# Four narrow merge-gate blocks as a twelfth block of the seven-product stage, with two more mLSTM heads' q and k in front of it

## The chip, the cores and the metric

The program runs on one core of a Trainium2 chip, in one launch. A core has engines that run side by side, each through its own list of instructions in order: TensorE (PE, matrix products into PSUM), VectorE (DVE), ScalarE (ACT), GpSimd (POOL) and SyncE (SP, which here only issues DMAs; ACT and POOL issue some too). They wait for each other through semaphores. The metric is the device time of one execution, in microseconds (us), lower is better.

## The reference, cut to what matters

A decoder layer with two token mixers side by side: 512 tokens, width 2048, all in float32. One projection of the normalised input `u` is cut into the inputs of both mixers and of the two merge gates:

```
u = _rmsnorm(h, norm_w)
proj = jnp.matmul(u, w_in)
(ml_q, ml_k, ml_v, ml_o, ml_z, ml_i, ml_f,
 dn_qkv, dn_z, dn_b, dn_a, gate_a, gate_b) = jnp.split(proj, idx, axis=-1)
h_a = _mlstm_chunkwise(q, k, v, i_pre, logf)         # 8 heads, q and k 128 wide, v 256 wide
h_a = _rmsnorm(h_a) * ml_norm_w * sigmoid(ml_o) * silu(ml_z)
h_b = _gated_delta_chunkwise(dq, dk, dv, beta, g)    # 16 heads of 128, after a causal conv and silu
h_b = _rmsnorm(h_b, dn_norm_w) * silu(dn_z)
y_a = jnp.matmul(h_a, w_out[:ML_WIDTH]); y_b = jnp.matmul(h_b, w_out[ML_WIDTH:])
return sigmoid(gate_a) * y_a + sigmoid(gate_b) * y_b  # added to h, then a last RMSNorm
```

`gate_a` and `gate_b` are 4096 columns of the projection; `ml_q` and `ml_k` are 1024 each.

## The kernel before, in words

Every large product is made of three: weights and `u` are split into a high part (rounded, `wh`, `uh`) and a rest (`wl`, `ul`), and high x high, high x rest and rest x high are added in PSUM. The split of a weight tile is one copy on ACT (`split_hi`, L136) and one subtraction on DVE (`split_lo`, L139). Weight tiles of 256 KB come in through the tag `wr` (four buffers, loads four tiles ahead, splits three ahead) in the order of the list `plan`.

There are three ways to project columns. `proj_cm` gives 256 columns as channels x tokens: 8 weight tiles, 96 matmuls that stream 512 columns each (L258 to L260). `proj_tm` gives 256 columns as tokens x channels: 8 weight tiles, 192 matmuls that stream 256 columns each (L273 to L276). `seven_stage` gives 1024 columns as tokens x channels with seven products of half-size blocks in place of eight: 336 matmuls that stream 512 columns each (L610 to L612), and on DVE and ACT the sums of weight blocks and of results that this needs. Its helper `sink_flat` puts the gates through tanh and stores them in `tg_d`.

The program's stages, in order on PE:

1. The front: `u` is made; mLSTM's q, then k, of heads 0 and 1 by `proj_cm` (stored in `qk_d` by `spill`); then the first two narrow merge-gate blocks (`narrow_gates`, `proj_tm`, 256 columns each). Beside them run `gates` (the small per-head gates), `u_sums` (sums of blocks of `u` for the seven products) and `lead` (the first weights of the next stage).
2. The seven-product stage: 11 blocks, listed in `SEVEN`: four `z`, two `s`, two `v`, three `g` (gates from column 1024 on).
3. The mixers: eight units (`dn_unit`), each two DeltaNet heads. A unit projects k, v and q of its heads (three `proj_cm` blocks); units 1 to 6 have one more `proj_cm` block behind k, which projects q and k of one mLSTM head (2 to 7) and starts `ml_head`. Heads 0 and 1 are started by `ml_first`, which loads q and k from `qk_d`.
4. The other two narrow merge-gate blocks, by `proj_tm`.
5. The output projection of `h_a`: four narrow `proj_tm` blocks (`n`), two wide blocks (`o`), and the seven-product stage again for `h_b` (two blocks).

PE's order is the order of the program. What runs beside the projections is written as generators: each calls for a pause of some steps, and a step passes with every 6 matmuls of `proj_cm` and every 12 of `proj_tm`, so that a block has 16 steps. `start(gen, wait)` sets the first step. The order on DVE, ACT, POOL and SP comes from a scheduler that takes priorities (`urgent`, `behind`) into account. Buffers limit it: an mLSTM head has one buffer each for q and k (`mkq`), for v and for its weights, and shares with the DeltaNet heads two buffers `g` for the gate.

What the change and the prediction touch, step by step:

- PSUM tag `pj` has three buffers and each `proj_cm` block takes two, so the second half of a block's first step needs the block before it copied out. For k, v and q of a unit that copy is `yp<-pj` on ACT (L831).
- `travel` (L867) stores transposed tiles by four DMAs of 64 KB; an mLSTM head stores its result `hm_d` by eight of them, a unit its `h_d` by eight per pair of heads, all on ACT's queue, in order with ACT's other work.
- `dn_front_k` inverts, on DVE, by 31 pairs of small operations (`tmp`, L942, and `xi`, L944); then the result goes through DRAM (`xd`, `tt`) and is transposed (`tn`, L960). 25 steps behind the end of the q block (9 where the unit has an mLSTM block) `dn_back` uses `tn` on PE (L998).
- `load_h` reads `hm_d` back in 16 tiles (`hr`, in the buffers of `wr`) and puts their high parts and rests into `uh` and `ul` (ACT L1238, DVE L1239), over those of `u`, for the output projection.
- `close` opens the buffers for the last stage when no generator is left; it is asked behind each `n` block.

## Time and profile before

| what | value |
|---|---|
| median of 3 runs | 2251.95 us (2249.82 to 2252.3) |
| the profiled execution's own time, as its span | 2252.6 us |
| DVE busy | 1658.0 us (74%) |
| ACT busy | 944.6 us (42%) |
| POOL busy | 294.0 us (13%) |
| front, to the first seven-product matmul | 0 to 126.7 us |
| seven-product stage, 11 blocks | 126.7 to 986.5 us |
| mixers, eight units | 986.5 to 1808.6 us |
| two narrow merge-gate blocks | 1808.6 to about 1864 us |

An execution of this program was taken with the hardware profiler; its span, from the first to the last instruction, is the time that the profile accounts for. Busy shares are per engine. A matmul's own duration in the profile overlaps the next one's, so PE's time per matmul is read from the distance of starts. "Idle before" is time in which an engine waited, with what ended the wait. The limits of the stages are starts of matmuls of the lines named above.

### The profile page before, as it was taken

The page shows a single profiled execution, that of the slowest core. Times are in us where ns is not written, and L with a number is a line of the kernel's source. Part 1 is how long each engine was busy: PE and PEld are TensorE (multiplying, and loading weights), DVE is VectorE, ACT ScalarE, POOL GpSimd, SP SyncE. Part 2 cuts the span into 40 slices and gives each one's busy share as a digit, 9 for nine tenths or more (in the row PEclk, how much of TensorE's full clock was granted, in tenths as well). Part 3 has the DMA queues.
Part 4 walks back from the last instruction along what each step waited for, and adds up shares of the span by engine and source line. Part 5 has one row for each costly group of instructions (what it writes and reads, how often), then busy time and mean ns, then how long its engine had stood idle before and what let it go on. Part 6 is the DMA issues. An engine that isn't in the chain of part 4 may idle for free. (4 is left out here: it accounts for less than half of the span.)

```text
span 2252.6 us, 33199 instructions
## 1 busy us (share of the span) xinstructions
PE 2183.0 (97%) x11408; PEld 1822.1 (81%) x11408; DVE 1658.0 (74%) x2911; ACT 944.6 (42%) x1824; POOL 294.0 (13%) x362
## 2 busy tenths in 40 slices
PE   7999999999999999998999999999999999999986
PEld 5987888788778778887888888888888899987765
DVE  5787888778877777857786777777767765747777
ACT  4444444445444444433434434343443443323334
POOL 0420000000000000012322131221222110000124
PEclk9999999999999999999999999999999999999988
DMA  5456666567667776767666665757666565958686
GB/s 159 129 166 198 212 202 209 191 194 239 201 202 225 229 222 189 247 195 181 154 162 152 145 167 131 176 136 172 138 167 147 134 172 171 284 155 258 206 238 243
DMA packets 541131, 422.27 MB, mean 187 GB/s; under 512 B 241441, under 2 KB 417794, under 8 KB 540962
## 3 DMA queue, kind: packets, MB, share of 16 engines
q1 hardware_dynamic: 443426, 358.20, 56.7%
q10 hardware_dynamic: 95744, 57.76, 8.4%
q0 software_dynamic: 1792, 4.20, 0.8%
q8 instruction: 89, 1.46, 0.3%
q14 instruction: 80, 0.66, 0.1%
HBM read 335.03 MB, written 85.00 MB: 186 GB/s over the span
## 5 line engine op out<-in xcount | busy, mean ns | idle before, releaser
L136 ACT CAST wh<-wr 128x512 fp32r<-128x512 f32 (+1 forms) x576 | 396.2, 690 | 554.1 <-PE pj L259 275.3
L139 DVE TENSOR_TENSOR wl<-wr,wh 128x512 fp32r<-128x512 f32 (+1 forms) x576 | 479.9, 836 | 178.7 <-ACT wh L136 168.6
L258 PE MATMUL pj<-uh,wh 128*128 128x512 f32 x1024 | 429.9, 420 | 5.5 <-ACT yp L831 5.5
L260 PE MATMUL pj<-uh,wl 128*128 128x512 f32 x1024 | 401.5, 392 | 0.0
L259 PE MATMUL pj<-ul,wh 128*128 128x512 f32 x1024 | 400.5, 391 | 0.0
L611 PE MATMUL ps<-wl,uh 128*128 128x512 f32 x592 | 234.0, 395 | 6.5 <-DVE wl L139 6.4
L610 PE MATMUL ps<-wh,uh 128*128 128x512 f32 x592 | 232.8, 393 | 6.0 <-DVE X L670 5.6
L612 PE MATMUL ps<-wh,ul 128*128 128x512 f32 x592 | 231.1, 390 | 0.0
L260 PEld LDWEIGHTS pj<-uh,wl 128*128 128x128 f32 x1024 | 192.8, 188 | 43.2
L258 PEld LDWEIGHTS pj<-uh,wh 128*128 128x128 f32 x1024 | 193.8, 189 | 40.5 <-ACT yp L831 5.9
L259 PEld LDWEIGHTS pj<-ul,wh 128*128 128x128 f32 x1024 | 194.0, 189 | 33.1
L136 ACT CAST wh<-ts 128x512 fp32r<-128x512 f32 x200 | 123.4, 617 | 222.1 <-DVE ts L568 180.5
L136 ACT CAST wh<-t 128x1024 fp32r<-128x1024 f32 x104 | 109.5, 1053 | 245.1 <-PE ps L612 115.0
L611 PE MATMUL ps<-wl,suh 128*128 128x512 f32 x528 | 205.7, 390 | 0.5 <-DVE wl L139 0.5
L610 PE MATMUL ps<-wh,suh 128*128 128x512 f32 x528 | 205.9, 390 | 0.0
L612 PE MATMUL ps<-wh,sul 128*128 128x512 f32 x528 | 205.5, 389 | 0.0
L139 DVE TENSOR_TENSOR wl<-t,wh 128x1024 fp32r<-128x1024 f32 x104 | 132.0, 1269 | 42.7 <-ACT wh L136 42.0
L139 DVE TENSOR_TENSOR wl<-ts,wh 128x512 fp32r<-128x512 f32 x200 | 139.1, 699 | 31.3 <-ACT wh L136 31.3
L273 PE MATMUL pjt<-wh,uh 128*128 128x256 f32 x512 | 147.6, 288 | 0.8 <-ACT tgs L787 0.7
L275 PE MATMUL pjt<-wl,uh 128*128 128x256 f32 x512 | 144.8, 283 | 0.0
L276 PE MATMUL pjt<-wh,ul 128*128 128x256 f32 x512 | 144.8, 283 | 0.0
L611 PEld LDWEIGHTS ps<-wl,uh 128*128 128x128 f32 x592 | 111.4, 188 | 38.7 <-DVE wl L139 17.0
(321 smaller groups left out, 3845.1 us busy)
## 6 DMA issues: line engine op xcount, KB each, us to landing
wr<-in_w_in_dram SPq DMA_DIRECT2D x680, 256.0 KB, 3.7
wr<-in_w_out_dram SPq DMA_DIRECT2D x144, 256.0 KB, 4.3
t_d<-ts ACTq DMA_DIRECT2D x88, 256.0 KB, 4.3
wr<-t_d SPq DMA_DIRECT2D x88, 256.0 KB, 4.0
wr<-in_w_in_dram SPq DMA_DIRECT2D x96, 128.0 KB, 3.1
xt<-in_x_dram SPq DMA_DIRECT2D x8, 512.0 KB, 8.1
v<-v_d SPq DMA_DIRECT2D x8, 512.0 KB, 6.2
gb<-rows_d SPq DMA_DIRECT2D x16, 256.0 KB, 4.7
```

The lines of the kernel that those rows point to most:

```text
L136: newest["A"] = A.copy(hi, src).ins
L139: newest["V"] = V.tensor_tensor(out=lo, in0=src, in1=hi.bitcast(F32), op=ALU.subtract).ins
L258: T.matmul(ps[j], hi[:, k, wsl], uh[:, kt, :], start=(kt == 0), stop=False)
L259: T.matmul(ps[j], hi[:, k, wsl], ul[:, kt, :], start=False, stop=False)
L260: T.matmul(ps[j], lo[:, k, wsl], uh[:, kt, :], start=False, stop=(kt == KT - 1))
L273: T.matmul(o, uh[:, kt, tsl], hi[:, k, :], start=(kt == 0 and c % 2 == 0), stop=False, skip_group_check=True)
L275: T.matmul(o, uh[:, kt, tsl], lo[:, k, :], start=False, stop=False, skip_group_check=True)
L276: T.matmul(o, ul[:, kt, tsl], hi[:, k, :], start=False, stop=(kt == KT - 1), skip_group_check=True)
L610: T.matmul(ps[t], ah, hi, start=(g == "A" and i == 0), stop=False, skip_group_check=True)
L611: T.matmul(ps[t], ah, lo, start=False, stop=False, skip_group_check=True)
L612: T.matmul(ps[t], al, hi, start=False, stop=(i == KH - 1), skip_group_check=True)
```

## The change

The four narrow merge-gate blocks (gate columns 0 to 1023) are gone; `SEVEN` has a fourth `g` block, so that the seven-product stage has 12 blocks. In the front, where two of the narrow blocks stood, q and k of mLSTM heads 2 and 3 are projected by `proj_cm` and stored in `qk_d`. Units 1 and 2 have no mLSTM block any more; heads 2 and 3 are started by `ml_first` too, and the four heads of `ml_first` start at steps 1, 41, 81 and 121 of the mixers (before: two, at 1 and 45). The longer pause of head 2 (`late`) is gone. Behind the mixers PE goes straight to the `n` blocks, and `load_h` starts in front of the last unit's q block (before: in front of the last narrow gate block, two blocks later).

```diff
--- before.py
+++ after.py
@@ -24,8 +24,7 @@
 NRAW, NSPL = 4, 4
 RAHEAD, SAHEAD = 4, 3
 PRIO = 1500
-GFIRST = 2
-GNARROW = 4
+QKFIRST = 2
 YNARROW = 4
 GLAG = 8
 HP = S // 2
@@ -45,12 +44,12 @@
 NSYS = 32
 
 
-UNITS = [(p, p + 1 if 0 < p < 7 else None) for p in range(8)]
+UNITS = [(p, p + 1 if 2 * QKFIRST - 2 < p < 7 else None) for p in range(8)]
 
 SEVEN = ([("z", ML_Z + c, ML_O + c) for c in range(0, D, NO)]
          + [("s", DN_Z + c, DN_Z + c + NO) for c in range(0, D, 2 * NO)]
          + [("v", ML_V + c, ML_V + c + NO) for c in range(0, D, 2 * NO)]
-         + [("g", GATE + c, GATE + c + NO) for c in range(GNARROW * NB, 2 * D, 2 * NO)])
+         + [("g", GATE + c, GATE + c + NO) for c in range(0, 2 * D, 2 * NO)])
 
 
 @with_exitstack
@@ -86,7 +85,7 @@
     v_d = dr.tile([NC, P, D], F32, tag="vd", name="v_d")
     g_d = dr.tile([NC, P, D], F32, tag="gd", name="g_d")
     gz_d = dr.tile([NC, P, D], F32, tag="gzd", name="gz_d")
-    qk_d = dr.tile([4, P, S], F32, tag="qkd", name="qk_d")
+    qk_d = dr.tile([4 * QKFIRST, P, S], F32, tag="qkd", name="qk_d")
 
     ident = cp.tile([P, P], F32, tag="ident", name="ident")
     make_identity(nc, ident)
@@ -143,18 +142,13 @@
         return tc.issue_after(newest[eng])
 
 
-    def add_gates(blocks):
-        for b in blocks:
-            plan.extend(("i", GATE + b * NB, k) for k in range(0, KT, KP))
-
-    plan = [("i", c, k) for c in (ML_Q, ML_K) for k in range(0, KT, KP)]
-    add_gates(range(GFIRST))
+    QK = [(a, b) for b in range(QKFIRST) for a in range(2)]
+    plan = [("i", (ML_Q, ML_K)[a] + b * NB, k) for a, b in QK for k in range(0, KT, KP)]
     nfront = len(plan)
     for p, h in UNITS:
         for kind, c in (("i", DN_K + p * NB), ("m", h), ("i", DN_V + p * NB), ("i", DN_Q + p * NB)):
             if c is not None:
                 plan += [(kind, c, k) for k in range(0, KT, KP)]
-    add_gates(range(GFIRST, GNARROW))
     plan += [("n", b * NB, k) for b in range(YNARROW) for k in range(0, KT, KP)]
     plan += [("o", nb * NO, k) for nb in range(YNARROW * NB // NO, D // NO) for k in range(KT)]
     raws, parts = [], []
@@ -779,20 +773,11 @@
     lead, seven = seven_stage(sbp, (suh, sul), (s4h, s4l), X, t2_d, w_in, 0, SEVEN, SINK, begin_mixers)
 
 
-    def narrow_gates(b):
-        ps = proj_tm(GATE + b * NB)
-        for i in range(2):
-            tg = wp.tile([P, 2, NB], F32, tag="tg", name="tgs", bufs=3)
-            with urgent():
-                A.activation(tg, ps[i], AF.Tanh, scale=0.5)
-            nc.sync.dma_start(tg_d[2 * i:2 * i + 2, :, b * NB:(b + 1) * NB].rearrange("c p n -> p c n"), tg)
-
     start(gates())
     start(u_sums(), 11)
     start(lead(), 38)
-    spill(proj_cm(ML_K), 2, 1.0)
-    for b in range(GFIRST):
-        narrow_gates(b)
+    for a, b in QK[1:]:
+        spill(proj_cm((ML_Q, ML_K)[a] + b * NB), 2 * QKFIRST * a + 2 * b, 1.0 if a else float(P) ** -0.5)
     for b, blk in enumerate(SEVEN):
         seven(2 * KH * b, *blk)
     while active:
@@ -1112,13 +1097,15 @@
                 A.mul(mkq[:, 1, :], ps[0], float(P) ** -0.5)
             with urgent():
                 A.copy(mkq[:, 0, :], ps[1])
-            start(ml_head(mh, mkq, 16 if p == 1 else 0), 1)
+            start(ml_head(mh, mkq), 1)
         ps = proj_cm(DN_V + dcol)
         for j in range(2):
             vt = wk.tile([P, NC, P], F32, tag="vn", name="vt", bufs=4)
             u["vs"].append(vt)
             conv_silu(ps[j], 32 + hs[j], vt.rearrange("p c t -> p (c t)"))
             start(silu_end(vt.rearrange("p c t -> p (c t)"), (vt, vt)), 4 + 3 * j)
+        if p == UNITS[-1][0]:
+            start(load_h(hm_d, lambda k: 16 + k, 1, False), 4)
         ps = proj_cm(DN_Q + dcol)
         u["qn"] = []
         for j in range(2):
@@ -1129,7 +1116,7 @@
         start(dn_front_q(hs, kq, u), QWAIT)
         start(dn_back(hs, kq, u), 25 if mh is None else 9)
 
-    def ml_head(h, kq, late):
+    def ml_head(h, kq):
         kT, qT = kq[:, 0, :], kq[:, 1, :]
         kw = wk.tile([P, NC, P], F32, tag="mkw", name="kw", bufs=1)
         with behind("V"):
@@ -1162,7 +1149,7 @@
         v1 = wk.tile([P, NC, NB + 1], F32, tag="mv1", name="v1", bufs=1)
         G.memset(v1[:, :, NB:NB + 1], 1.0)
         nc.sync.dma_start(v1[:, :, 0:NB], v_d[:, :, h * NB:(h + 1) * NB].rearrange("c p n -> p c n"))
-        yield 6 + late
+        yield 6
         with behind("V"):
             V.tensor_tensor(out=kw, in0=kw, in1=bc(we, P), op=ALU.mult)
         yield 2
@@ -1217,18 +1204,10 @@
 
         kq = wk.tile([P, 2, S], F32, tag="mkq", name="mkq", bufs=1)
         for i in range(2):
-            nc.sync.dma_start(kq[:, 1 - i, :], qk_d[2 * i + h])
+            nc.sync.dma_start(kq[:, 1 - i, :], qk_d[2 * QKFIRST * i + h])
         yield 4
-        yield from ml_head(h, kq, 0)
-
-    start(ml_first(0), 1)
-    start(ml_first(1), 45)
-    for unit in UNITS:
-        dn_unit(*unit)
-
-
-
-    hh, hl = {0: uh}, {0: ul}
+        yield from ml_head(h, kq)
+
     y_d = dr.tile([NC, P, D], F32, tag="yd", name="y_d")
 
     def load_tile(dst, src):
@@ -1247,10 +1226,10 @@
             split_scaled(uh[:, k, 0:n], ul[:, k, 0:n], raw[:, 0:n], normc[:, norm(k):norm(k) + 1])
             yield step
 
-    for b in range(GFIRST, GNARROW):
-        if b == GNARROW - 1:
-            start(load_h(hm_d, lambda k: 16 + k, 1, False), 4)
-        narrow_gates(b)
+    for h in range(2 * QKFIRST):
+        start(ml_first(h), 1 + 40 * h)
+    for unit in UNITS:
+        dn_unit(*unit)
 
     h1s, h2s = ctx.enter_context(ExitStack()), ctx.enter_context(ExitStack())
     late = {}
```

ACT at the third mLSTM head's store. Before, this is head 2 (the one of unit 1), while unit 2 runs; the `w` are copies of the DeltaNet chain, `mkq` takes q and k of the next head out of PSUM:

```order
L867 DMA hm_d<-to 32x16x32
L1062 COPY w<-pw 128x128
L867 DMA hm_d<-to 32x16x32 x2
L1062 COPY w<-pw 128x128
L867 DMA hm_d<-to 32x16x32
L136 CAST wh<-wr 128x512
L867 DMA hm_d<-to 32x16x32 x4
L136 CAST wh<-wr 128x512 x2
L1062 COPY w<-pw 128x128
L1112 ACTIVATE mkq<-pj 128x512
L1062 COPY w<-pw 128x128
```

Now it is head 2 again, now in unit 2, beside `dn_back` of unit 1 (`tb`, `s`):

```order
L852 DMA hm_d<-to 32x16x32
L1001 COPY tb<-p_11494 32x8x32 x2
L852 DMA hm_d<-to 32x16x32 x2
L135 CAST wh<-wr 128x512
L852 DMA hm_d<-to 32x16x32
L1008 ACTIVATE s_11565<-p_11556 64x512
L852 DMA hm_d<-to 32x16x32 x2
L816 COPY yp_9094<-pj 128x512
L852 DMA hm_d<-to 32x16x32
L135 CAST wh<-wr 128x512
L816 COPY yp_9096<-pj 128x512
L852 DMA hm_d<-to 32x16x32
```

The eight stores have the copies `yp<-pj` of a unit's v block among them, where a copy of q and k of an mLSTM head stood behind all eight.

DVE in the last unit's inversion, beside the copies of its q block (`kq`, `yp`). Before:

```order
L832 TENSOR_SCALAR kq_16800<-yp_8630,convc 128x512
L944 TENSOR_TENSOR xi<-xi,tmp 128x5x14
L834 SCALAR_TENSOR_TENSOR kq_16800<-yp_8630,convc,kq_16800 128x512
L942 TENSOR_TENSOR tmp<-ls,xi 128x65
L139 TENSOR_TENSOR wl<-wr,wh 128x512
L834 SCALAR_TENSOR_TENSOR kq_16800<-yp_8630,convc,kq_16800 128x512
L832 TENSOR_SCALAR kq_16801<-yp_8632,convc 128x512
L944 TENSOR_TENSOR xi<-xi,tmp 128x5x13
L834 SCALAR_TENSOR_TENSOR kq_16800<-yp_8630,convc,kq_16800 128x512
L834 SCALAR_TENSOR_TENSOR kq_16801<-yp_8632,convc,kq_16801 128x512
```

Now the same part of the inversion's surroundings:

```order
L1218 SCALAR_TENSOR_TENSOR ul<-hr,normc,uh 128x512
L929 TENSOR_TENSOR xi<-xi,tmp 128x4x19
L817 TENSOR_SCALAR kq_16958<-yp_9096,convc 128x512
L819 SCALAR_TENSOR_TENSOR kq_16957<-yp_9094,convc,kq_16957 128x512
L1218 SCALAR_TENSOR_TENSOR ul<-hr,normc,uh 128x512
L927 TENSOR_TENSOR tmp<-ls,xi 128x72
L138 TENSOR_TENSOR wl<-wr,wh 128x512
L819 SCALAR_TENSOR_TENSOR kq_16958<-yp_9096,convc,kq_16958 128x512
L819 SCALAR_TENSOR_TENSOR kq_16957<-yp_9094,convc,kq_16957 128x512
L1218 SCALAR_TENSOR_TENSOR ul<-hr,normc,uh 128x512
L929 TENSOR_TENSOR xi<-xi,tmp 128x4x18
L1218 SCALAR_TENSOR_TENSOR ul<-hr,normc,uh 128x512
```

The rests of `load_h` (`ul`) stand inside the inversion, two or more for each weight tile (`wl`). Its end, before:

```order
L942 TENSOR_TENSOR tmp<-ls,xi 128x8
L944 TENSOR_TENSOR xi<-xi,tmp 128x8
L139 TENSOR_TENSOR wl<-wr,wh 128x512 x2
L960 STREAM_TRANSPOSE tn<-tt 128x256
L139 TENSOR_TENSOR wl<-wr,wh 128x512
L1239 SCALAR_TENSOR_TENSOR ul<-hr,normc,uh 128x512
```

and now:

```order
L927 TENSOR_TENSOR tmp<-ls,xi 128x16
L929 TENSOR_TENSOR xi<-xi,tmp 128x8x2
L927 TENSOR_TENSOR tmp<-ls,xi 128x8
L929 TENSOR_TENSOR xi<-xi,tmp 128x8
L138 TENSOR_TENSOR wl<-wr,wh 128x512
L842 STREAM_TRANSPOSE qn<-kq_16958 128x512
L138 TENSOR_TENSOR wl<-wr,wh 128x512
L945 STREAM_TRANSPOSE tn<-tt 128x256
L138 TENSOR_TENSOR wl<-wr,wh 128x512 x2
L966 TENSOR_SCALAR qe<-qe 128x8
```

Before, `load_h` begins behind the transposition `tn`. Now its 16 operations are ahead, and a transposition of `qn` stands between the inversion's end and `tn`.

## Prediction

> **What bounds the kernel now.** I read the page's busy shares first, then its 40 slices, then PE's list of waits, then starts of matmuls.
>
> ```profile
> PE 2183.0 (97%) x11408; PEld 1822.1 (81%) x11408; DVE 1658.0 (74%) x2911; ACT 944.6 (42%) x1824; POOL 294.0 (13%) x362
> ...
> PE   7999999999999999998999999999999999999986
> ```
>
> ```profile
> PE ps L611 <- DVE wl L139: 8.3, 17, 1.4
> ...
> PE pj L258 <- ACT yp L831: 5.5, 1, 5.5
> PE ps L610 <- DVE ty L1342: 5.1, 1, 5.1
> ...
> PE p L1009 <- ACT s L1003: 1.2, 2, 1.0
> ```
>
> TensorE is busy in all slices but the first and the last two, and its waits between the ends are few: the time is the sum of matmuls. So the change is priced by matmuls saved, less the waits that appear where PE's work gets shorter and the work beside it does not. How long a matmul holds PE is the distance of starts, not its printed duration. Two pairs of rows, 42 streams of 512 columns apart, and 21 of 256 apart:
>
> ```profile
> 58.60 0.40 PE L258 MATMUL pj<-uh,wh 128*128 128x512 f32 x1
> ...
> 68.14 0.39 PE L258 MATMUL pj<-uh,wh 128*128 128x512 f32 x1
> ```
>
> ```profile
> 79.06 0.28 PE L273 MATMUL pjt<-wh,uh 128*128 128x256 f32 x1
> ...
> 81.58 0.28 PE L273 MATMUL pjt<-wh,uh 128*128 128x256 f32 x1
> ```
>
> 9.54 / 42 = 0.227 us, and 2.52 / 21 = 0.120 us. A narrow stream costs a little over half a wide one.
>
> **The change part by part.**
>
> *Four narrow blocks removed.* 4 x 192 matmuls x 0.120 = 92.2 us of PE.
>
> *A twelfth seven-product block.* The 11 blocks of before start at the first row below; the first `proj_cm` matmul behind them is in the second.
>
> ```profile
> L610 PE MATMUL ps<-wh,suh x528: 387/389/504, 126.7 to 953.2; 128*128 128x512 f32 x176
> ...
> ```
>
> ```profile
> L258 PE MATMUL pj<-uh,wh x48: 389/389/479, 986.5 to 1019.4; 128*128 128x512 f32 x48
> ```
>
> (986.5 - 126.7) / 11 = 78.2 us for a block. Its 336 matmuls alone are 336 x 0.227 = 76.3; the other 1.9 are waits for `wl` and `X`, which the new block, a `g` like the last three, will have too. Its sums, its second read of half the weights through DRAM and its tanh work are inside that figure. Net on PE: -92.2 + 78.2 = -14.0 us. Nothing hides TensorE's own time, so this term lies on the path whole.
>
> *A rule that speaks against this size.* The Trainium skill, "TensorE: Matmul & The Clock Gate", section "Part 1: The HAM clock gate", gives a warm matmul N / 2.4 GHz plus about 2.5 ns. As an estimate from that page the narrow blocks would be 768 x 0.109 = 83.8 and the wide ones 336 x 0.216 = 72.5, and the gain 11.3, or 9.4 with the same 1.9 of waits. The rows above show about 13 ns on top of N / 2.4 GHz at either width, so the trace does not agree, and I keep 14.0.
>
> *Two more heads' q and k moved to the front.* Two blocks of 96 matmuls, 2 x 21.8 us, at both places: 0 on PE. The two units that lose their mLSTM block get shorter by 21.8 us each and keep the rest of their work. Four `spill` stores on ACT's queue and four `mkq` loads on SP are new (256 KB each); against them stand eight `tg_d` stores that leave SP. In the front the work beside PE stays while PE gives up 2 x 23.0 and takes on 2 x 21.8:
>
> ```profile
> 78.00:126.00 48.00, 48.00 (x405) 47.52 (x404) 37.98 (x49) 20.66 (x38) 26.24 (x26) 1.00 0.46 138
> ...
> 1278.00:1387.00 109.00, 109.00 (x627) 91.39 (x627) 80.34 (x195) 44.17 (x117) 27.40 (x34) 1.00 0.66 155
> ```
>
> (Columns behind the length: PE, its weight loads, DVE, ACT, POOL, clock, DMA share.) In the front DVE has 38.0 of 48 us: 2.4 us less room still leaves over 7. I take 0, with +3 as the end above. In a unit with an mLSTM block DVE has 80.3 of 109; without the block's 8 splits (0.68 each, the row below) it has 75 of 87, or 86%. That fits, but closely.
>
> ```profile
> L139 DVE TENSOR_TENSOR wl<-wr,wh 128x512 fp32r<-128x512 f32 x16 | 10.9, 682 | 2.2 <-ACT wh L136 2.2
> ```
>
> *Handover from one early head to the next.* The one long wait of the mixers stands where head 0 hands over to head 1:
>
> ```profile
> 1058.47 0.89 ACTq L867 DMA_DIRECT2D hm_d<-to  x2
> 1059.48 0.62 ACT L136 CAST wh<-wr 128x512 fp32r<-128x512 f32 x1 [4.37 <-PE pj L260]
> 1062.36 3.90 ACTq L867 DMA_DIRECT2D hm_d<-to  x3
> 1066.31 0.58 ACT L831 COPY yp<-pj 128x512 f32<-128x512 f32 x1 [6.21 <-DMA v<-v_d]
> ...
> ```
>
> ```profile
> 1066.95 0.80 PE L258 MATMUL pj<-uh,wh 128*128 128x512 f32 x1 [5.47 <-ACT yp L831]
> ...
> ```
>
> ```profile
> 1056.00:1078.00 22.00, 16.53 (x62) 13.12 (x61) 16.70 (x41) 5.60 (x12) 0.10 (x1) 0.84 0.87 205
> ```
>
> The `yp` copy is due 1.4 us (6 matmuls) behind the end of a block, and stood behind five `hm_d` issues on ACT's queue, which in turn waited for slow landings (DMA share 0.87, while the next head's `v`, gates, q and k are loaded). PE lost 5.5 us, and the clock, 0.84 over 22 us, another 3.5: 9.0 in all. The change has four such heads for two. Head 0's store stays where it was, with four issues ahead of the copy for five. By the order, head 1's store has no `yp` inside it; head 2's has six issues ahead of the `yp` of unit 2's v block; head 3's has a `dn_back` copy. The seven later stores of before, with other copies behind them, left no such wait (one `pj <- yp` in the whole list). So the new price lies between 0 and 2 x 9.0 = 18. I take +2.5, nearer to the lower end: the new `yp` comes at a place where the first stores can leave some steps before the block ends.
>
> *The last unit, and `load_h`.* The cover of two blocks behind the last unit is gone, but `dn_back` and its chain keep their steps: four `n` blocks have 64 steps, as the two gate blocks and two `n` blocks had. What moves is `load_h`: from the second gate block into the last unit's q block, where DVE runs the inversion.
>
> ```profile
> 1788.00:1829.00 41.00, 40.72 (x264) 36.69 (x263) 38.12 (x107) 14.41 (x37) 7.35 (x6) 1.00 0.69 159
> ```
>
> ```profile
> L1239 DVE SCALAR_TENSOR_TENSOR ul<-hr,normc,uh 128x512 fp32r<-128x512 f32 x16 | 12.1, 754 | 16.9 <-ACT uh L1238 16.8
> ```
>
> ```profile
> 1828.68 0.18 DVE L944 TENSOR_TENSOR xi<-xi,tmp 128x8 f32<-128x8 f32 x1
> ...
> 1836.67 0.45 DVE L960 STREAM_TRANSPOSE tn<-tt 128x256 f32<-128x256 f32 x1 [4.27 <-DMA tt<-xd]
> ```
>
> ```profile
> 1846.79 0.69 PE L998 MATMUL p<-tn,aq 32*32 32x32 f32 x32
> ...
> ```
>
> DVE has 2.9 us free in these 41. The order puts all 16 rests (12.1 us) and two gate products (2 x 0.7, as long as a split) inside the inversion, so its end moves from 1828.9 by 13.5 less about 2 of free time, to about 1840.5. The way through DRAM takes 1836.7 - 1828.9 = 7.8 us, so `tn` is done at about 1848.8; the transposition of `qn`, new between the two, waits for a buffer of the other `qn` and can make it later. PE wants `tn` at 1846.8: a wait of 2 us, of which the 1.2 at `s` (list of waits) is saved. Against that the first `n` block wants the splits and `uh` from a DVE that is late by up to the whole backlog; a PE that waits there also comes later to `tn`, so the two do not add fully. I take +4 for both, about midway; the ends are 0 (the backlog absorbed) and +10 (the 13.5 less the free 2 and the saved 1.2).
>
> *Queues.* `load_h` is moved past SP's loads of the last unit; its tiles share four `wr` buffers with the weights, and 16 tiles took 39 us before, against 28 steps of 109 / 64 = 1.7 us, or 47 us, from its start to the end of the first `n` block. No loss taken, but it is inside the +10. The work behind `close` (`h_sums`) moves from `n` blocks to an `o` block, where DVE is over half free (second fence):
>
> ```profile
> L1238 ACT ACTIVATE uh<-hr,normc x16: 707/722/725, 1838.7 to 1877.2; 128x512 fp32r<-128x512 f32 x16
> ```
>
> ```profile
> 1974.00:1996.00 22.00, 22.00 (x99) 18.22 (x98) 8.61 (x12) 6.07 (x11) 0.00 (x0) 1.00 0.57 184
> ```
>
> *Sum.* -14.0 + 0 + 2.5 + 4 = -7.5 us. The profiled execution spans 2252.6, 0.65 above the median of the runs (2251.95); against its own time the sum gives 2245.1, against the runs 2244.4.
>
> **The rivals.**
>
> 1. *Slower: each handover stalls PE.* If ACT's queue holds the `yp` copies at two more handovers as it did at the first, 2 x 9.0 replaces 2.5: -14.0 + 18.0 + 4 = +8, 2260. For it: DMA share 0.87 and a third unit in a row without the block that gave room. Against it: stores in mid-block cost nothing. It decides once the two new waits cost over 7.3 us each, clock included (-14.0 + 4 + 14.6 = +4.6).
> 2. *About no change: DVE becomes the bound from the last unit's q block to `tn`.* If the waits there come to +10 and the handovers to +3, the sum is -1: 2251. For it: 38.1 busy of 41 before 12 us are added. Against it: the loads of `load_h` start early, and PE reaches `tn` only 9 steps into the second `n` block.
> 3. *Full gain.* Waits stay as they are, or head 0's even shrinks: -14.0, 2238.
> 4. *The matmul rule named above.* As a mechanism here, narrow and wide streams with a smaller common overhead would save 9.4, less 6.5 of waits: 2249. The rows of before are against it.
>
> **How the numbers follow.** A measurement of this kernel can tell about 0.2%, 4.5 us, from no change. Forecast (between -12 and -4.5): 0.50; rival 3: 0.10; rival 2: 0.14; rival 1: 0.23; rival 4: 0.03. Faster is the forecast and rival 3, 0.60; within 0.2% are rivals 2 and 4, 0.17; slower is rival 1, 0.23. The range runs from 2237 (all of the 14.0, and a wait less) to 2261 (rival 1 in full); past it I leave some 5% below and 12% above. The forecast alone has 2240 to 2247.5.
>
> **What the profile after would show.** Right: half as many 256-wide matmuls; 12 seven-product blocks at 78 us each; at most one handover with PE waiting for `yp` over 3 us; `tn` of the last unit done 2 to 6 us behind the moment PE wants it; DVE over 90% from the last q block into the first `n` block. Wrong: several waits `pj <- yp` of 4 us and more with the clock under 0.9 beside them (rival 1); PE waiting for `wl` or `uh` through the first `n` block (rival 2); a twelfth block much above 78 us, or a late first seven-product block, would break the first term.

## The result, and the profile after

The change makes the kernel slower by about 0.3 to 0.4%, where 0.33% faster was forecast. It was compared with the kernel before twice:

| comparison | before, us | after, us | ratio, 95% interval |
|---|---|---|---|
| first | 2249.82 (9 runs) | 2257.64 (9 runs) | 1.0027 (1.0017 to 1.0037) |
| second, with the experiments | 2252.66 (28 runs) | 2262.18 (7 runs) | 1.0041 (1.0025 to 1.0057) |

Two executions of after were profiled. The first spans 2252.3 us and lies among the fastest runs of its comparison; the second spans 2260.4 and lies at the median of its own. I read the second, and name the first where they differ. Its page begins:

```profile
PE 2174.6 (96%) x10976; PEld 1798.7 (80%) x10976; DVE 1700.6 (75%) x2953; ACT 958.7 (42%) x1834; POOL 298.4 (13%) x362
...
PE   7999999999999999999999999999999998999986
```

TensorE is busy 8.4 us less than before. Of the 40 slices one points at a loss: the 34th (1865 to 1921), behind the last unit, is at 8, where before has its one 8 of the middle in the 19th, at the handover. A tenth of a slice is 5.7 us, too coarse for sizes. Starts of matmuls give them. These are the stage limits (seven-product stage, mixers, `n` blocks, last stage):

```profile
L604 PE MATMUL ps<-wh,suh x576: 389/389/502, 124.7 to 1026.6; 128*128 128x512 f32 x192
```

```profile
L252 PE MATMUL pj<-uh,wh x896: 387/393/793, 1061.1 to 1846.0; 128*128 128x512 f32 x180
```

```profile
L267 PE MATMUL pjt<-wh,uh x256: 277/283/561, 1846.7 to 1970.6; 128*128 128x256 f32 x128
```

```profile
L604 PE MATMUL ps<-wh,tuh x96: 387/389/794, 2062.2 to 2202.2; 128*128 128x512 f32 x96
```

and the last limit in the kernel before:

```profile
L610 PE MATMUL ps<-wh,tuh x96: 388/389/797, 2055.5 to 2194.9; 128*128 128x512 f32 x96
```

| stage, us | before | after, 1st profile | after, 2nd | by matmuls alone | 2nd, over that |
|---|---|---|---|---|---|
| front | 126.7 | 123.9 | 124.7 | -2.5 | +0.5 |
| seven-product, 11 or 12 blocks | 859.8 | 937.1 | 936.4 | +78.2 | -1.6 |
| mixers | 822.1 | 782.1 | 785.6 | -43.6 | +7.1 |
| from the last unit to the last stage | 246.9 | 212.0 | 215.5 | -46.1 | +14.7 |
| last stage to the end | 197.1 | 197.2 | 198.2 | 0 | +1.1 |

So the 14.0 us of matmuls were saved, and 21.8 came back: a third in the mixers, two thirds behind the last unit. In the first profile it is +3.6 and +11.2 at the same two places. Every run's time on record is some 2 us above its span (2254.1 and 2252.3 in the first profile), so the profiled execution of before, 2252.6 as a span, was itself some 2.5 us slower than the median of its runs (2251.95), and differences from it come out that much too small. PE's waits between the end of the last q block and 1960, in the second profile (us in total, times, longest):

```profile
PE pqk L953 <- DVE kq L826: 3.5, 1, 3.5
PE pjt L267 <- ACT yp L816: 3.3, 1, 3.3
PE pw L1044 <- DVE tb L1014: 3.3, 1, 3.3
PE p L994 <- ACT s L988: 0.9, 2, 0.7
```

Before had 4.0 us of waits in five small groups there, from 1808.6 to 1960, and this was the longest:

```profile
PE pr L1051 <- DVE st L1070: 1.5, 1, 1.5
```

Behind each of the long ones the granted clock falls (third column from the right):

```profile
1846.00:1866.00 20.00, 16.21 (x115) 15.49 (x114) 17.09 (x40) 10.13 (x16) 0.00 (x0) 0.91 0.85 230
1866.00:1886.00 20.00, 16.49 (x126) 16.29 (x125) 15.84 (x45) 5.59 (x10) 1.29 (x1) 0.91 0.57 160
1912.00:1932.00 20.00, 16.73 (x120) 16.53 (x120) 7.11 (x13) 2.91 (x6) 0.00 (x0) 0.83 0.56 176
```

That is at most 20 x (0.09 + 0.09 + 0.17) = 7.0 us of clock on top of 11 of waits (at most, since PE still stood idle for a part of the slow stretches). And the mixers:

```profile
PE pj L252 <- ACT yp L816: 4.0, 1, 4.0
PE pw L1044 <- DVE r L1039: 3.4, 2, 1.7
PE pnum L1163 <- DVE c L1173: 1.3, 1, 1.3
PE pk L887 <- DVE kq L826: 1.3, 1, 1.3
PE p L1012 <- ACT s L1008: 0.8, 1, 0.8
```

One long wait for `yp`, at the first handover, as before (5.5 there). What is new are short waits: 4.3 us between 1140 and 1319, in the two units that lost their block, and 4.0 between 1319 and 1548, in units 3 and 4, which kept theirs. The clock lost as much as before: 0.94 over 1126.5 to 1140 and 0.87 over 1140 to 1160 are 3.4 us, and 0.83 over 1060 to 1080 in before is 3.4 too.

### The profile page after: what moved, and what is told of

Same layout as the page of the kernel before. It is cut to its first block, busy times and chain, and to the rows that moved or that the text cites. A ratio compares the mean times of both kernels' runs of the same rounds, so it can differ in the third digit from the quotient of the medians.

```text
span 2252.3 us, 32412 instructions
## 1 busy us (share of the span) xinstructions
PE 2171.1 (96%) x10976; PEld 1797.4 (80%) x10976; DVE 1699.0 (75%) x2953; ACT 956.4 (42%) x1834; POOL 298.6 (13%) x362
## 5 line engine op out<-in xcount | busy, mean ns | idle before, releaser
L605 PE MATMUL ps<-wl,uh 128*128 128x512 f32 x640 | 252.4, 394 | 5.8 <-DVE wl L138 5.7
L604 PE MATMUL ps<-wh,uh 128*128 128x512 f32 x640 | 251.2, 393 | 5.8 <-DVE X L664 4.1
L606 PE MATMUL ps<-wh,ul 128*128 128x512 f32 x640 | 249.8, 390 | 0.0
L605 PE MATMUL ps<-wl,suh 128*128 128x512 f32 x576 | 224.5, 390 | 1.7 <-DVE wl L138 1.7
L604 PE MATMUL ps<-wh,suh 128*128 128x512 f32 x576 | 224.8, 390 | 0.9 <-ACT qk L363 0.5
L606 PE MATMUL ps<-wh,sul 128*128 128x512 f32 x576 | 224.4, 390 | 0.0
L138 DVE TENSOR_TENSOR wl<-ts,wh 128x512 fp32r<-128x512 f32 x216 | 151.1, 703 | 33.6 <-ACT wh L135 33.6
L604 PEld LDWEIGHTS ps<-wh,uh 128*128 128x128 f32 x640 | 120.7, 189 | 35.9 <-DVE X L664 8.9
L550 DVE TENSOR_TENSOR t<-wr 128x1024 f32<-128x1024 f32 x112 | 137.2, 1225 | 7.4 <-DMA wr<-in_w_in_dram 6.9
L562 DVE TENSOR_TENSOR ts<-wr 128x512 f32<-128x512 f32 x104 | 71.7, 690 | 92.8 <-DMA wr<-t_d 73.9
```

The source lines that it names most:

```text
L138: newest["V"] = V.tensor_tensor(out=lo, in0=src, in1=hi.bitcast(F32), op=ALU.subtract).ins
L550: V.tensor_tensor(out=t13, in0=r[:, 1:3, :], in1=r[:, 0:2, :], op=ALU.subtract)
L562: V.tensor_tensor(out=ts[:, 0, :], in0=r[:, 0, :], in1=r[:, 2, :], op=ALU.subtract)
L604: T.matmul(ps[t], ah, hi, start=(g == "A" and i == 0), stop=False, skip_group_check=True)
L605: T.matmul(ps[t], ah, lo, start=False, stop=False, skip_group_check=True)
L606: T.matmul(ps[t], al, hi, start=False, stop=(i == KH - 1), skip_group_check=True)
```

## The experiments

Every kernel ran beside the kernel before on the same chip, and the chips differ from call to call, so ratios to before are compared; 0.1% is 2.25 us. "Below after" means below the +9.2 of r5; against the first comparison's 1.0027 (+6.1) each such gain is 3.1 smaller.

| kernel | ratio to before, 95% | in us |
|---|---|---|
| after, again (r5) | 1.0041 (1.0025 to 1.0057) | +9.2 |
| tail alone (e1) | 1.0047 (1.0032 to 1.0061) | +10.6 |
| heads alone (e2) | 1.0009 (0.9998 to 1.0019) | +2.0 |
| after without the twelfth block (r13) | 1.0098 (1.0082 to 1.0114) | +22.1 |
| after without `load_h` (r12) | 0.9988 (0.9976 to 1.0000) | -2.7 |
| after, half the loads of `load_h` (r6) | 1.0019 (1.0006 to 1.0031) | +4.3 |
| stores on SP's queue (e3) | 1.0030 (1.0018 to 1.0041) | +6.8 |
| own buffers for gate tiles (e4) | 1.0024 (1.0011 to 1.0038) | +5.4 |
| unit 6's stores later (r7) | 1.0034 (1.0023 to 1.0045) | +7.7 |
| three tail mends (r8) | 1.0034 (1.0017 to 1.0051) | +7.7 |
| rests partly on GpSimd, tail (r10) | 1.0020 (1.0008 to 1.0032) | +4.5 |
| rests partly on GpSimd, units 1, 2 (r9) | 1.0052 (1.0032 to 1.0072) | +11.7 |
| both of these (r11) | 1.0043 (1.0030 to 1.0055) | +9.7 |
| inversion later (r14) | 1.0048 (1.0034 to 1.0062) | +10.8 |
| head 0's stores later (r16) | 1.0037 (1.0023 to 1.0052) | +8.3 |
| all mends (r15) | 1.0042 (1.0026 to 1.0058) | +9.5 |
| DVE work left out of units 1, 2 (r17) | 1.0038 (1.0025 to 1.0052) | +8.6 |
| before, head 0's stores later (r18) | 1.0000 (0.9988 to 1.0011) | 0.0 |

Of the variants of after only r12 (below) and r13 (above) have intervals clear of those of after itself (1.0017 to 1.0057 over its two comparisons). No kernel is faster than the kernel before by more than its interval; r12, which leaves work out, just reaches 1.0000.

### The parts of the change

*The tail alone (e1).*

```diff
-GFIRST = 2
+GFIRST = 4
...
+        if p == UNITS[-1][0]:
+            start(load_h(hm_d, lambda k: 16 + k, 1, False), 4)
         ps = proj_cm(DN_Q + dcol)
...
-        if b == GNARROW - 1:
-            start(load_h(hm_d, lambda k: 16 + k, 1, False), 4)
```

> The kernel before with its tail alone changed as in the kernel after: all four narrow gate blocks stand in the front, no block stands between the last unit and the n blocks, and the reading back of hm_d starts in front of the last unit's q block. Eleven seven-product blocks and the two early heads stay, so PE has the same matmuls as before. Tail theory (the loss is in the last unit and the first two n blocks): by the two profiles this stretch and the n blocks took 258.1 us after, two narrow blocks added, against 246.9 before, so about +11 against the kernel before (+8 to +15). Handover theory (the loss is in the early heads): 0 to +4.

Measured +10.6 us (7.2 to 13.8). PE's waits there are of the same kinds as in after:

```profile
PE pqk L968 <- DVE kq L841: 2.7, 1, 2.7
PE pjt L273 <- ACT yp L831: 2.5, 1, 2.5
PE p L1009 <- ACT s L1003: 2.0, 2, 1.9
```

*The heads alone (e2).* The front, `UNITS`, `qk_d` and `ml_first` as in the change's diff, on the kernel before; `GFIRST`, `GNARROW` and `SEVEN` stay.

```diff
-UNITS = [(p, p + 1 if 0 < p < 7 else None) for p in range(8)]
+UNITS = [(p, p + 1 if 2 * QKFIRST - 2 < p < 7 else None) for p in range(8)]
...
-    start(ml_first(0), 1)
-    start(ml_first(1), 45)
+    for h in range(2 * QKFIRST):
+        start(ml_first(h), 1 + 40 * h)
```

> The kernel before with its early heads alone changed: q and k of heads 2 and 3 are projected in the front, units 1 and 2 have no mLSTM block, the four heads start at 1, 41, 81 and 121. Narrow gate blocks, seven-product stage and tail stay, so PE has the same matmuls as before. Tail theory: +3 to +6, since the mixers took 782.1 us after, with 43.6 added for the two blocks 825.7, against 822.1 before. Handover theory: +14 or more, most of the loss, with several waits of PE for yp and the clock under 0.9 beside them.

Measured +2.0 us (-0.5 to +4.3), with one wait for `yp` (2.3 us) in the mixers: no second handover stalls. The short waits of after are there too (`r` 3.0 in two, `c` 2.0, `kq` 1.0), so they come with the early heads.

*After again (r5), without an edit.*

> The kernel after, unchanged, beside the kernel before on the chip of the other experiments. If the change is the sum of its parts (tail alone +10.0, heads alone +2.4, twelfth block for four narrow ones -14.0), it is -2 to 0 against before here. If the parts hurt each other or the twelfth block saves less than 14.0, it is +5 to +9, as in the first comparison (+7.8).

Measured +9.2 us (5.6 to 12.8): 10.6 + 2.0 - 14.0 = -1.4 is not this.

*After without the twelfth block (r13).*

```diff
+GFIRST = 4
+GNARROW = 4
...
-         + [("g", GATE + c, GATE + c + NO) for c in range(0, 2 * D, 2 * NO)])
+         + [("g", GATE + c, GATE + c + NO) for c in range(GNARROW * NB, 2 * D, 2 * NO)])
...
+    for b in range(GFIRST):
+        narrow_gates(b)
     for b, blk in enumerate(SEVEN):
```

> The kernel after without the twelfth block: the four narrow gate blocks stand in the front behind q and k of the four heads, eleven seven-product blocks; mixers and tail are those of after. If the swap of four narrow blocks for a twelfth one is worth its matmuls, this kernel is 11 to 15 us above after, about +20 to +24 against before, and the parts (tail, heads) hurt more together than alone. If the parts add as measured alone, it is +12 against before, only 3 above after, and the swap saves little.

Measured +22.1 us (18.5 to 25.7) against before. Against after's +9.2 the swap is worth 12.9, near the 14.0 of the sum. Against the first comparison's +6.1 it would be 16.0. Tail and heads together cost 22.1 by the runs, where alone they cost 10.6 and 2.0, on other chips. The profiles, one execution each, say otherwise. By stages, over before and with the matmuls that moved taken out (46.1 for two narrow blocks, 43.6 for two `proj_cm` blocks):

| stage, us | tail alone (e1) | heads alone (e2) | both (r13) |
|---|---|---|---|
| front | -0.1 | +2.8 | +2.6 |
| seven-product, 11 blocks | -1.9 | -3.1 | -0.5 |
| mixers | -1.4 | +2.5 | +2.4 |
| from the last unit to the last stage | +12.4 | +0.4 | +11.9 |
| last stage to the end | -2.8 | +0.3 | +0.6 |

At the three places that the edits touch (front, mixers, behind the last unit) the two cost 16.9 us together and 16.6 alone, so the profiles show no place where they hurt each other. What differs stands in the two other stages, whose code is the same in all three, and between the runs' 22.1 and the profiles' 17.0. Whether the two cost more together stays open.

### The reading back of hm_d

*After without `load_h` for `h_a` (r12).*

```diff
-        if p == UNITS[-1][0]:
-            start(load_h(hm_d, lambda k: 16 + k, 1, False), 4)
```

> The kernel after without load_h for h_a: hm_d is never read back, and the output projection of h_a uses u in its place (16 loads of 256 KB, 11.6 us of ACT and 12.1 us of DVE are left out; PE has the same matmuls). If the tail's loss comes from load_h inside the last unit, the waits for yp, kq and tb go with their clock: 9 to 14 us less than after, that is 0 to 5 us below before. If it comes from the missing cover of two blocks itself (the last unit's own chain stands beside n blocks), the waits stay in part and the gain is under 5 us.

Measured -2.7 us against before, 11.9 below after by the ratios, so the gain of the first reading came. From the last unit to the last stage it takes 2054.2 - 1847.0 = 207.2 us, in place of 215.5 and 212.0 in the two profiles of after; 246.9 - 46.1 = 200.8 would be no loss, so 6.4 us stay there without `load_h`. Of the waits only the one for `kq` is gone, as the second reading has it:

```profile
PE pw L1044 <- DVE tb L1014: 3.2, 1, 3.2
PE pjt L267 <- ACT yp L816: 2.3, 1, 2.3
```

So both readings have a part. No run leaves `load_h` out of the kernel before, so what it costs at its old place is not measured.

*Half of its loads (r6).*

```diff
-            raw = wp.tile([P, S], F32, tag="wr", name="hr", bufs=NRAW)
-            load_tile(raw, src[k])
+            if halves or k % 2 == 0:
+                raw = wp.tile([P, S], F32, tag="wr", name="hr", bufs=NRAW)
+                load_tile(raw, src[k])
```

> The kernel after, with every second tile of hm_d left out: load_h reads 8 tiles from DRAM in place of 16 and puts each through ACT and DVE twice, so ACT and DVE have the same work and the DMAs half of it (the output projection of h_a then uses half of the heads' columns twice). If the tail's loss is contention of the DMAs (late hr tiles and late landings of stores, in front of the yp copies on ACT's queue), the waits of PE for yp (3.1 us) and for kq (2.7 us) and the clock under 0.9 behind them go: 6 to 9 us less than after. If the loss is DVE's 12 us of added work, all of it stays: the time of after within 2 us.

Measured 4.9 us below after by the ratios, with overlapping intervals. The wait for `yp` stays at 3.2, that for `kq` falls to 1.7. By the runs the DMAs are some 40% of the 11.9 us that `load_h` costs. By the profiles they are nearly all of it: from the last unit to the last stage r6 takes 2054.6 - 1846.6 = 208.0 us, as r12 without `load_h`. But the profiled execution of r6 is one of its fastest (2251.83, the median is 2255.99), so how much is the DMAs' and how much DVE's and ACT's stays open.

### Why the copies are late, and what happens when one wait is mended

ACT's instructions at the end of the last q block in after (start, length, and in brackets the idle time before, with what ended it):

```profile
1844.91 1.46 ACT L1217 ACTIVATE uh<-hr,normc 128x512 fp32r<-128x512 f32 x2 [2.70 <-DMA hr<-hm_d]
1845.65 0.31 ACTq L852 DMA_DIRECT2D h_d<-to  x1
1847.44 0.62 ACT L135 CAST wh<-wr 128x512 fp32r<-128x512 f32 x1 [1.07 <-DMA wr<-in_w_out_dram]
1847.46 3.45 ACTq L852 DMA_DIRECT2D h_d<-to  x4
1850.95 0.59 ACT L816 COPY yp<-pj 128x512 f32<-128x512 f32 x1 [2.89 <-DMA h_d<-to]
```

The copy stands behind four issues of `h_d` that hold the queue for 3.45 us, and these behind `uh`, which wait for tiles of `load_h` (2.70). It is the handover's mechanism, at a place where the prediction did not look for it.

*The stores on SP's queue (e3).*

```diff
-        q = nc.scalar if out else nc.sync
+        q = nc.sync
```

> The kernel after with the stores of hm_d and h_d issued from SP's queue and no longer from ACT's. If the yp copies are late because they stand behind these stores, the waits of PE for yp go (3.1 us in front of the first n block with 3.5 of clock behind it, 2.8 us at 1134): 6 to 10 us less than after, so about -2 to +2 against the kernel before. If the copies are late for another reason, or the stores on SP's queue hold up the loads of weights instead, the time is that of after (about +8 against before) or more.

+6.8 us, no gain that can be told. ACT is free of the stores, and the copy now stands behind a `uh` that waits for its tile:

```profile
1848.92 0.72 ACT L1217 ACTIVATE uh<-hr,normc 128x512 fp32r<-128x512 f32 x1 [1.07 <-DMA hr<-hm_d]
1849.55 0.57 ACT L816 COPY yp<-pj 128x512 f32<-128x512 f32 x1
```

PE's wait there falls from 3.3 to 2.4; the wait for `yp` in the mixers goes, and one for `c` of 5.0 us comes.

*Unit 6's stores later (r7).* `turn` and `travel` of unit 6's results wait seven steps more.

```diff
-        turn(g, h_d[h], True)
+        turn(g, h_d[h], True, 7 if h // 2 == 6 else 0)
```

> The kernel after, with the eight h_d stores of unit 6 seven steps later, so that on ACT's queue they stand behind the yp copies of the last q block and not ahead of them; load_h as in after, its uh still ahead of the copies. If the stores alone hold the copies up, the wait of 3.1 us and its clock go: 5 to 7 us less than after. If the uh behind late hr tiles hold them up as well, a wait of 2 us or more stays, and the gain is under 3 us.

+7.7 us: 1.5 below after, and a wait for `yp` of 2.8 stays, as the second reading has it: with the stores gone, the copy stands behind two `uh`, which wait 1.71 us for late tiles. But late tiles alone are not the cause either. In r12, without `load_h`, the copy waits 2.03 us for stores of `h_d`, and PE 2.3. Each of the two is enough, and no run took both away.

*Own buffers for the first gate tiles (e4).*

```diff
-            tg = wp.tile([P, 2, NB], F32, tag="tg", name="tgn", bufs=3)
+            if b == 0:
+                tg = wk.tile([P, 2, NB], F32, tag=("mkw", "mw")[i], name="tgn", bufs=1)
+            elif b == 1 and "sb" not in late:
+                tg = both[:, i, :].rearrange("p (c n) -> p c n", c=2)
+            else:
+                tg = wp.tile([P, 2, NB], F32, tag="tg", name="tgn", bufs=3)
```

> The kernel after with buffers of their own (those of the mLSTM heads, idle by then) for the gate tiles tgn of the first two n blocks, which share three buffers with the last unit's qn otherwise. If the last waits of the tail (second qn late, tn late, DVE standing at the n blocks' ends while tb waits) come from that sharing, tn is ready some us earlier and the wait of 2.6 us for tb goes with its 1.8 of clock: about 4 us less than after, +3 to +4 against before. If DVE is late only by the work of reading back hm_d, nothing changes: +8 against before.

+5.4 us. The wait for `tb` is gone as expected (it came from DVE standing for tiles of the `n` blocks' ends that share three buffers with `qn`), a wait of 1.2 for `tn` has appeared, and that for `yp` is 4.6 in its profile. No kernel with these buffers (e4, r8, r10, r11, r15) waits over 0.3 us for `tb` at this place. A gain of 3.8 by the ratios, inside the intervals.

*Three tail mends (r8)*: e4 and r7, and `load_h` five steps later.

```diff
-            start(load_h(hm_d, lambda k: 16 + k, 1, False), 4)
+            start(load_h(hm_d, lambda k: 16 + k, 1, False), 9)
```

> The kernel after with three edits of its tail: the stores of unit 6 seven steps later, load_h started five steps later (9 in place of 4), and gate tiles of the first two n blocks in buffers of their own. If the loss sits in the tail's three waits (yp, kq, tb) and the clock behind them, most of 9.8 us comes back: 6 to 10 us less than after, and then this kernel is faster than before by up to 8 us. If hr tiles are now too late for the first n block, a wait for uh or ul stands at its start, and the time is that of after or more.

+7.7 us. The waits for `yp` and `kq` are about 1.1 us shorter each, and `tn` is now what PE waits for:

```profile
PE p L983 <- DVE tn L945: 6.8, 1, 6.8
PE pqk L953 <- DVE kq L826: 2.4, 1, 2.4
PE pjt L267 <- ACT yp L816: 2.1, 1, 2.1
```

*Rests partly on GpSimd (r10)*: e4, r7, and

```diff
+            if k % 2 and not halves:
+                A.activation(raw, raw, AF.Copy, scale=w)
+                A.copy(uh[:, k], raw)
+                G.tensor_tensor(out=ul[:, k], in0=raw, in1=uh[:, k].bitcast(F32), op=ALU.subtract)
```

> The kernel after with three edits of its tail: the stores of unit 6 seven steps later, gate tiles of the first two n blocks in buffers of their own, and the rests (ul) of every second tile of load_h computed on GpSimd, behind one more scaling on ACT; load_h starts where it did in after. If DVE's 12 us inside the inversion make tn and kq late, half of it gone takes 1 to 2 us off each of the waits for kq and tn and the clock loss behind them: with the buffers 6 to 9 us less than after. If the DMAs set the pace (halved loads gave 6.2 less), the gain is that of the buffers alone, 3 to 4 us.

+4.5 us, the best of the variants of after that leave nothing out: 4.7 below it by the ratios, though the intervals overlap, and still slower than before. No wait for `tn` or `tb`; `kq` 4.2 in two waits, `yp` 2.8.

### The shortened units

*DVE relieved by GpSimd (r9).* Every third `wl` of units 1 and 2:

```diff
+        if pool:
+            G.tensor_tensor(out=lo, in0=src, in1=hi.bitcast(F32), op=ALU.subtract)
+            return
```

> The kernel after, with the rest (wl) of every third weight tile of units 1 and 2 computed on GpSimd in place of VectorE, 16 of 48 operations of 0.7 to 0.8 us, so that DVE has some 12 us less in the two units that lost their mLSTM block. If the small waits of these units (pw<-r, pnum<-c, pk<-kq, p<-s, 7 to 8 us together between 1200 and 1400 in the second profile of after) come from a DVE that is late, about half of them goes: 3 to 5 us less than after. If they come from DMAs that land late (DMA share 0.75 to 0.97 there), the time stays within 1.5 us of after.

+11.7 us: no gain, and PE now waits 5.3 us for `c`. The relief did not relieve: DVE's busy time in the two units is 149.0 us for 150.7 in r5, though some 12 us of work had left it. An operation of DVE takes 0.74 us alone and 1.78 beside one of GpSimd (`mkq`); the small `xi`, 0.22 in r5's mean, takes 1.32 beside a `wl` that was moved:

```profile
1148.53 0.74 DVE L823 SCALAR_TENSOR_TENSOR kq<-yp,convc,kq 128x512 f32<-128x512 f32 x1
...
1149.94 1.78 DVE L823 SCALAR_TENSOR_TENSOR kq<-yp,convc,kq 128x512 f32<-128x512 f32 x1
1151.64 1.32 DVE L933 TENSOR_TENSOR xi<-xi,tmp 128x66 f32<-128x66 f32 x1
```

```profile
1149.44 1.72 POOL L1151 TENSOR_TENSOR mkq<-mkq,iwb 128x512 f32<-128x512 f32 x1 [2.98 <-DVE tmp L931]
1151.30 1.57 POOL L139 TENSOR_TENSOR wl<-wr,wh 128x512 fp32r<-128x512 f32 x1
```

The Trainium skill, "SBUF — State Buffer", section "SBUF: two separate sides", says that VectorE and GpSimd share a pair of ports as an exclusive lock (for an operation of VectorE with two inputs in SBUF, as here, only against one of GpSimd that reads SBUF): who starts first has it for a whole instruction, the other stands. The trace agrees to 0.2 us: 0.74 behind GpSimd's end at 1151.16 is 1151.90, and the operation of 1.78 ended at 1151.72.

*Both reliefs (r11)*, r9 and r10 together, no further edit.

> The edits of the two kernels above together (rests of units 1 and 2 partly on GpSimd; stores later, own buffers, every second ul on GpSimd). If the two places are independent, the gains add: 9 to 13 us less than after, and then 0 to 4 us less than before. If the late DVE is not what holds PE, it stands where the better of the two stands.

+9.7 us: between the two.

*The inversion later (r14).* In r5 DVE stands in order for the inversion's load, with `r` behind it, for which PE waits:

```profile
1297.93 0.28 DVE L1055 COPY st<-pst 128x128 f32<-128x128 f32 x1
1303.05 0.19 DVE L927 TENSOR_TENSOR tmp<-ls,xi 128x31 f32<-128x31 f32 x1 [4.83 <-DMA ls<-ld]
...
1304.05 0.34 DVE L1039 SCALAR_TENSOR_TENSOR r<-pr,negeg,vt 128x128 f32<-128x128 f32 x1
```

```diff
-        yield 7
+        yield 10 if hs[0] // 2 in (2, 3) else 7
         for i in range(BS - 1):
```

> The kernel after with the inversion of units 2 and 3 started three steps later (10 in place of 7 behind its loads). If PE's waits for r in these units (3.4 us together, with up to 2 us of clock) come from DVE standing in order for ls<-ld (4.8 and 5.0 us there) with r behind it, they go: 3 to 5 us less than after. If they come from somewhere else, or tn is now late for dn_back, the time is that of after or more.

+10.8 us, and `r` is still waited for (4.1 us in two waits). The scheduler set the operation where it stood before, with DVE waiting for its load at the same place:

```profile
1302.71 0.19 DVE L927 TENSOR_TENSOR tmp<-ls,xi 128x31 f32<-128x31 f32 x1 [5.35 <-DMA ls<-ld]
```

So this run tells nothing of the cause: that PE waits for `r` because DVE stands for `ls` is read from the order of the two rows, not shown by an experiment.

*DVE work left out (r17)*: two of three added taps of the convolution in units 1 and 2.

```diff
+        taps = (2,) if p in (1, 2) else (2, 1, 0)
...
-        for j in (2, 1, 0):
+        for j in taps:
```

> The kernel after with two of the three added taps of the causal convolution left out in units 1 and 2 (24 operations of 0.78 us on DVE, 9.4 us in each unit; q, k and v of these heads are then wrong), everything else as in after. If DVE is what the two shortened units wait for (75 us of work and 6 us of standing for DMAs in 89), PE's small waits there (6 to 8 us with the clock) go: 4 to 7 us less than after. If the DMAs' round trips set the pace, the waits stay and the time is within 2 us of after.

+8.6 us. DVE's busy time in the two units falls by 12.6 us:

```profile
1140.00:1229.20 89.20, 88.61 (x518) 72.79 (x518) 77.17 (x186) 36.80 (x95) 23.67 (x32) 0.97 0.69 164
1229.20:1319.00 89.80, 85.98 (x522) 71.23 (x520) 73.56 (x188) 38.04 (x109) 31.07 (x34) 1.00 0.71 172
```

(after) and

```profile
1140.00:1229.00 89.00, 84.17 (x500) 69.42 (x500) 70.85 (x179) 36.71 (x93) 24.98 (x32) 0.98 0.72 171
1229.00:1319.00 90.00, 89.61 (x543) 74.81 (x544) 67.25 (x170) 39.26 (x111) 26.31 (x34) 1.00 0.75 181
```

The waits for `c` and `s` are gone, `r` has 2.9 us in place of 3.4, `tb` 1.3 in place of 0.3, and one for `st` of 1.4 is new. DVE's load is part of what makes these waits, but taking it away gives no time that can be told.

*Head 0's stores later (r16).*

```diff
-            turn(g[i], hm_d[2 * h + i], True)
+            turn(g[i], hm_d[2 * h + i], True, 5 if h == 0 else 0)
```

> The kernel after with head 0's eight hm_d stores five steps later, behind the yp copies of unit 1's k block on ACT's queue. If the store's place holds the copies up, PE's wait for yp at the first handover (2.8 to 4.0 us) goes with the clock behind it: 3 to 6 us less than after. If the copies or the blocks behind them then wait for something else (v of the next head, DVE's transpositions that need the buffer of the stores), the gain is under 2 us.

+8.3 us. The 4.0 us for `yp` are gone; `pqk` waits 1.4 for `kq` and `pnum` 2.9 for `c` in their place.

*All mends (r15)*: r10, r14 and r16 together, no further edit.

> All mends together: own buffers for the first gate tiles, every second rest of load_h on GpSimd, stores of unit 6 and of head 0 later, inversion of units 2 and 3 later. If the places are independent, the gains add up to 10 to 13 us less than after, 0 to 4 us below before. If a wait mended at one place comes back at the next, it stays 2 to 6 us above before.

+9.5 us, no better than after. The gains do not add.

*Before, with head 0's stores later (r18)*: the edit of r16 on the kernel before.

> The kernel before with head 0's eight hm_d stores five steps later, behind the yp copies of unit 1's k block. If the wait of 5.5 us and the clock at 0.84 behind it are worth the 9.0 us that the prediction gave them, this kernel is 5 to 9 us faster than before, and then faster than both kernels. If the copies then wait for something else (as in after, where this edit gained about 1 us), it is within 2 us of before.

No change (-2.7 to +2.5 us). The 5.5 us for `yp` and the clock of 0.83 at 1060 to 1080 are gone, and PE waits in the same unit for others, 1.7 us for `kq` in two waits and 2.8 for `c`, with the clock at 0.91 behind it:

```profile
PE pnum L1176 <- DVE c L1184: 2.8, 1, 2.8
```

```profile
1060.00:1080.00 20.00, 18.28 (x92) 15.11 (x91) 18.97 (x48) 6.25 (x13) 2.67 (x3) 1.00 0.94 226
1098.00:1118.00 20.00, 17.21 (x156) 13.74 (x155) 15.10 (x41) 11.56 (x33) 8.66 (x10) 0.91 0.61 138
```

## Why the prediction was wrong, point by point

- *"Net on PE: -92.2 + 78.2 = -14.0 us"*: right. Twelve blocks take (1061.1 - 124.7) / 12 = 78.0 each, and r13 puts the swap at 12.9 us. The matmul rule's 11.3 or 9.4 lies inside that run's uncertainty, so the experiment does not decide between the two prices.
- *The front, 0*: right (+0.5; +2.8 and +2.6 in e2 and r13, within its end of +3).
- *Handover, +2.5*: one wait for `yp` over 3 us in the mixers, as forecast, and rival 1 did not happen at the handovers. The wait even fell, from 5.5 to 4.0 us with the same loss of clock. But the step "in a unit without the block it has 75 of 87 ... That fits, but closely", priced at 0, failed: the two shortened units took 89.2 and 89.8 us, and with the short waits there and in the two units behind them the mixers stand at +7.1 (+3.6 in the first profile, +2.5 in e2, +2.4 in r13). A busy share of 86% leaves out that DVE also stands in order for DMAs, 4.8 us for `ls` alone. The kernel before showed such standing already, 7.6 us in a whole unit (1291.4 to 1400.0):

```profile
DVE tn L960 <- DMA tt<-xd: 5.4, 1, 5.4
DVE tmp L942 <- DMA ls<-ld: 2.2, 1, 2.2
```

- *The last unit, +4 with the ends 0 and +10*: this is the step that failed most. It measured +14.7 and +11.2 in the two profiles of after, +12.4 in e1 and +11.9 in r13, past the upper end each time. The sum followed DVE's backlog to `tn`. PE did not wait for `tn` at all (it was done at 1892.5, and PE, late itself, came to it at 1895.9), but ahead of it for `yp` and `kq` and behind it for `tb`. Left out were the stores of unit 6 on ACT's queue; priced at no loss were late tiles of `load_h` and the cover of two blocks ("`dn_back` and its chain keep their steps"). `load_h` is worth 8.3 us of this stage against the second profile (r12; 11.9 over the whole program by the ratios), and 6.4 stay without it. The clock, up to 7.0 us, was given to the handover and not to this place. "DVE over 90%" was wrong too: 17.09 of 20.
- *The rivals*: rival 2 had the right place, and +10 there with +3 at the handovers; with +14.7 and +7.1, as in the profile at the median, it comes out slower, not even. Its row, 38.1 of 41 busy, was the warning. PE did not wait for `wl` or `uh` through the first `n` block, as that rival had it (0.4 us).
- *The 9.0 us of a handover* was used as a price, and r18 shows that the wait has no such price: taken away, most of its time is found again in the same unit, and the kernel is no faster.
- *"0.65 above the median"* compares a span with run times; the profiled execution was some 2 us further above the runs, as said with the result. This moves no term of the sum.

So a size was wrong at the tail, and a term put at nothing in the units beside the early heads. Under both lies one reading: PE's list of waits was taken for what the side work costs, and the absence of waits for room.

## What to carry to other kernels

Matmuls saved are saved, but where they were the cover of a chain through DVE, ACT and DRAM, price that chain against what is left of PE's time, with the time in which an engine stands in order for a DMA, before the saving is booked. A single long wait of PE is no price: mend it and the next late link takes its place; none of the mends tried on after could be told from the unmended kernel, and only leaving out the reading back of `hm_d`, the chain's own work, could. Two edits that touch such a chain are worth a run together: these two cost 12.6 us apart and 22.1 together by the runs, though the stages of the profiles show no place where they hurt each other.

## What the hardware showed that I had not expected

The clock falls in steps. Behind waits of 2.5 to 5 us the granted clock is often 0.91 or 0.83 over 20 us, that is 1.8 or 3.4 us lost, once or twice. Narrower windows show a clock of 0.50 for a short stretch, here behind the wait of 3.3 us for `yp` in the second profile and, in the first, behind one of only 1.7 us for `kq` that ended at 1361.6:

```profile
1851.90:1855.20 3.30, 3.30 (x18) 3.30 (x17) 3.30 (x8) 2.80 (x5) 0.00 (x0) 0.50 1.05 269
```

```profile
1362.10:1365.40 3.30, 3.30 (x12) 2.81 (x12) 0.45 (x2) 2.32 (x7) 0.00 (x0) 0.50 1.26 176
```

The Trainium skill, "TensorE: Matmul & The Clock Gate", section "Part 1: The HAM clock gate", has half the clock after an idle window of 3413 ns that runs free of the program, until a busy window; half of 3.4 is 1.7, which agrees with the step. The traces do not agree with the condition: a whole idle window does not fit into a wait of 1.7 us. With a free window it would fit that a wait of 2.8 us at 1134.6 in the first profile cost nothing (1.00, first row) and one of 3.1 at 1844 did (0.83, second):

```profile
1135.00:1155.00 20.00, 17.23 (x88) 14.65 (x89) 17.03 (x46) 6.92 (x14) 4.94 (x4) 1.00 0.93 211
1843.00:1863.00 20.00, 16.68 (x116) 16.23 (x115) 16.90 (x39) 10.33 (x17) 0.00 (x0) 0.83 0.84 230
```

It would also make runs of one kernel differ by steps of some 2 us; that was not tried.

A store's issue on ACT's queue can end with the landing of a load that SP issued. At the first handover of after (second profile) the second of the two issues below and the copy behind it were released by the landing of `v` of the next head, as the profile infers from the semaphores:

```profile
1134.28 4.21 ACTq L852 DMA_DIRECT2D hm_d<-to  x2
1138.54 0.59 ACT L816 COPY yp<-pj 128x512 f32<-128x512 f32 x1 [5.08 <-DMA v<-v_d]
```
